# adaLN products of a float32 transformer trunk on VectorE and GpSimd with sums on ScalarE, weight transfers queued behind the main weights, and hidden activations in a ring of seven blocks

## The chip, the cores and the metric

The kernel runs on one core of a Trainium2 chip. The metric is the device time of one execution in microseconds (us), median over runs. TensorE (PE) does the matrix products, VectorE (DVE), ScalarE (ACT) and GpSimd (POOL) the elementwise work, and SyncE (SP) issues most transfers.

## The reference

Two layers of a diffusion transformer step, all in float32, on 384 tokens of width 1024. Each layer adds a gated half-step FFN, a mixer (differential attention, latent attention, a state-space scan called S5) and a second half-step FFN. Shift, scale and gate of each come from the adaLN product, a vector times a 1024 x 9216 matrix for each of two condition vectors:

```python
def adaln(cvec, l, p):
    m = jax.nn.silu(cvec) @ p['w_ada'][l] + p['b_ada'][l]
    return m.reshape(cvec.shape[0], N_MOD, D_MODEL)

def trunk_layer(x, mod, l, p, pos, ctx):
    sh1, sc1, g1, sh2, sc2, g2, sh3, sc3, g3 = [mod[:, i, None, :] for i in range(N_MOD)]
    nw = p['norm_w'][l]
    x = x + 0.5 * g1 * swiglu(modulate(rms_norm(x, nw[0]), sh1, sc1), p['ffn_w_in'][l, 0], p['ffn_w_out'][l, 0])
    m, new_ctx = mixer(modulate(rms_norm(x, nw[1]), sh2, sc2), l, p, pos, ctx)
    x = x + g2 * m
    x = x + 0.5 * g3 * swiglu(modulate(rms_norm(x, nw[2]), sh3, sc3), p['ffn_w_in'][l, 1], p['ffn_w_out'][l, 1])
    return x, new_ctx
```

`trunk_layer` runs for the prompt's 128 tokens with `c_ctx` and for the sample's 256 with `c`; the kernel takes both groups together, so each modulation has two columns.

## The kernel before

Activations lie transposed, 128 partitions x 8 blocks x 384 tokens. Every large product is exact to float32 by a split in two: ScalarE copies a weight block to `whi` (rounded), VectorE subtracts to get `wlo`, and `mm3` does three matmuls, whi x hi, whi x lo, wlo x hi. There are three buffers for raw weights and two for each split half, so a split can run at most one half block ahead of its matmuls. Weights come by SyncE, 1 MB at a time.

An FFN has 22 "up" blocks and 16 "down" blocks. An up block is two half blocks of 24 matmuls; behind it `up_post` copies a bias (`bb`), multiplies by the norm (`t`, out of PSUM), applies SiLU and the gate product (`sl`, ScalarE and VectorE in turn), and splits the result into `hidh` and `hidl`. Up and down alternate by `QUARTERS`: twelve ups, four downs, five ups, four downs, five ups, eight downs. The last downs of a stage also make the norm and the input of the next.

The adaLN products are cut into 64 units of 1 MB of weights (the first 8 MB are made in the start, apart). `ada_steps` makes them as steps in a list, `fillers`, and `fill` pops one after each up or down or attention step. A unit before is a load in SyncE's queue into one of the `raw` buffers and a run of small float32 matmuls on TensorE with the 2-column condition `conds` (`adaps`, L293); at the end of a group the sums are transposed (`adapt`) and added into `adaT`. Together with them, in the first FFN of a layer pair, go the steps of `s5_prep` (tables `big`, `Otab`, on VectorE and GpSimd). GpSimd otherwise does some `wlo` in the mixers. The units stand thus: 12 in the first FFN (called FFN00 here), 32 in mixer 0, 2 in FFN01 and 2 in FFN10 (second FFN of layer 0, first of layer 1), 16 in mixer 1, none in FFN11.

A scheduler of the framework puts the instructions of each engine into one fixed order; an engine runs its own list strictly in that order.

Of the kernel before, what the change touches and what calls it, by code (L numbers as in the profile page):

```python
# [31 lines left out]
YB = 8  # L32
# [33 lines left out]
def _layout(inp):  # L66
# [5 lines left out]
    wa = w[:, :, :8192].reshape(2, 8, 128, 4, 2048).transpose(0, 3, 1, 2, 4).reshape(2, 32, 128, 2048)  # L72
    wb = w[:, :, 8192:].reshape(2, 4, 2, 128, 1024).transpose(0, 1, 3, 2, 4).reshape(2, 4, 128, 2048)
    d['wada'] = np.concatenate([wa, wb], 1)
    for z in range(2):
        wc = w[:, :, 4096 + 1024 * z:5120 + 1024 * z].reshape(2, 4, 2, 128, 1024).transpose(0, 1, 3, 2, 4)
        d['wada'][:, 16 + 4 * z:20 + 4 * z] = wc.reshape(2, 4, 128, 2048)
    d['wada'][0, :8] = w[0, :, :2048].reshape(8, 128, 2, 8, 128).transpose(3, 1, 0, 2, 4).reshape(8, 128, 2048)
# [98 lines left out]
def trunk(ctx, tc, I, O):  # L177
# [100 lines left out]
    def ada_steps(l, g):  # L278
        w = 512 if g in (0, 1, 3) else 256
        units = w // 64  # L280
        row = int(8 * g)
        st = {}

        def unit(u):
            raw = load(I['wada'][l, row + u])
# [156 lines left out]
    def ffn(l, i, h, norm, gate, after, quiet=0, started=()):  # L442
        hh, hl = h
        fp = cur['fp']
        with cur['stack']:
            hq = {}

            def new_quarter(q):
                hq[q] = (fp.tile([128, 6, NT], FR, tag="hidh", name="hidh", bufs=2),
                         fp.tile([128, 6, NT], FR, tag="hidl", name="hidl", bufs=2))  # L450

            st = {}

            def up_post(j, ps):
                q = [n for n, (a, c) in enumerate(QUARTERS) if a <= j < a + c][0]
                if q not in hq:
                    new_quarter(q)
                dh, dl = hq[q]
                jj = j - QUARTERS[q][0]
# [39 lines left out]
            def down(q, m2):  # L499
# [4 lines left out]
                dh, dl = hq[q]  # L504
                for z in range(2):
                    w = split(raw[:, :, z, :], n, 128)
                    for k in range(n):
                        mm3(ps[z][:, :NT], w[0][:, k, :], w[1][:, k, :], dh[:, k, :], dl[:, k, :],
                            k == 0, k == n - 1)
# [1017 lines left out]
```

## Time and profile before

| | before |
|---|---|
| median of 3 runs | 1704.24 us (1701.77 to 1705.44) |
| the profiled execution's own time | 1711.13 us |
| span of its trace | 1708.8 us |
| PE busy | 1662.6 us, 97% |
| DVE busy | 1100.3 us, 64% |
| ACT busy | 690.3 us, 40% |
| POOL busy | 158.0 us, 9% |

A busy share is over the whole span; the span lies a few microseconds under the execution's own time, the rest being start and end of the program. The stages of the trace: start until 50 us, FFN00 to 340, mixer 0 to 594, FFN01 to 888, FFN10 to 1171, mixer 1 to 1413, FFN11 to 1696.

### The profile page before, as it was taken

The page shows a single profiled execution, that of the slowest core. Times are in us where ns is not written, and L with a number is a line of the kernel's source. Part 1 is how long each engine was busy: PE and PEld are TensorE (multiplying, and loading weights), DVE is VectorE, ACT ScalarE, POOL GpSimd, SP SyncE. Part 2 cuts the span into 40 slices and gives each one's busy share as a digit, 9 for nine tenths or more (in the row PEclk, how much of TensorE's full clock was granted, in tenths as well). Part 3 has the DMA queues.
Part 4 walks back from the last instruction along what each step waited for, and adds up shares of the span by engine and source line. Part 5 has one row for each costly group of instructions (what it writes and reads, how often), then busy time and mean ns, then how long its engine had stood idle before and what let it go on. Part 6 is the DMA issues. An engine that isn't in the chain of part 4 may idle for free.

```text
span 1708.8 us, 26147 instructions
## 1 busy us (share of the span) xinstructions
PE 1662.6 (97%) x10144; PEld 1502.8 (88%) x10144; DVE 1100.3 (64%) x2752; ACT 690.3 (40%) x1295; POOL 158.0 (9%) x220
## 2 busy tenths in 40 slices
PE   7999999999999999999999999999999999999997
PEld 6888999998545899999999999999964589999997
DVE  5974576757456788587576555557844766555555
ACT  4332343533455533333344333335234654333333
POOL 1210110013001400000000000001301040000000
PEclk9999999999999999999999999999998999999999
DMA  9564542544457443354253343435345123333432
GB/s 377 189 217 165 137 149 96 160 157 142 172 225 278 152 155 133 110 140 136 87 172 141 120 138 109 139 99 178 135 151 188 37 94 129 124 124 111 136 102 83
DMA packets 45931, 251.47 MB, mean 147 GB/s; under 512 B 5600, under 2 KB 10576, under 8 KB 23920
## 3 DMA queue, kind: packets, MB, share of 16 engines
q1 hardware_dynamic: 41360, 241.12, 40.9%
q0 software_dynamic: 2144, 4.54, 1.1%
q10 hardware_dynamic: 2304, 4.15, 0.8%
q8 instruction: 79, 1.29, 0.3%
q14 instruction: 44, 0.36, 0.1%
HBM read 246.73 MB, written 3.05 MB: 146 GB/s over the span
## 4 chain that ended last, share of the span: by engine, by line
PE 89%; DVE 5%; DMA 2%; ACT 2%; issue 1%; POOL 0%; SPq 0%; DVEq 0%; ACTq 0%
PE up L239 14%; PE up L241 14%; PE up L240 14%; PE down L241 7%; PE down L239 7%; PE down L240 7%; PE adaps L293 4%; PE pj L239 2%; PE sc L1208 2%; PE pj L241 2%; PE pj L240 2%; PE wtp L1165 1%; PE pout L239 1%; PE pout L241 1%; PE pout L240 1%
## 5 line engine op out<-in xcount | busy, mean ns | idle before, releaser
L234 ACT ACTIVATE whi<-raw 128x1024 fp32r<-128x1024 f32 (+3 forms) x360 | 332.5, 925 | 661.6 <-PE up L240 335.6
L239 PE MATMUL up<-hh,whi 128*128 128x386 f32 x1408 | 474.7, 342 | 7.8 <-ACT whi L234 4.0
L241 PE MATMUL up<-hh,wlo 128*128 128x386 f32 x1408 | 479.3, 341 | 0.7 <-DVE wlo L213 0.6
L240 PE MATMUL up<-hl,whi 128*128 128x386 f32 x1408 | 479.1, 341 | 0.0
L213 DVE TENSOR_TENSOR wlo<-raw,whi 128x1024 fp32r<-128x1024 f32 (+2 forms) x318 | 347.8, 1094 | 50.0 <-ACT whi L234 47.2
L239 PEld LDWEIGHTS up<-hh,whi 128*128 128x128 f32 x1408 | 266.5, 190 | 15.6 <-ACT whi L234 5.3
L241 PEld LDWEIGHTS up<-hh,wlo 128*128 128x128 f32 x1408 | 266.2, 189 | 9.4 <-DVE wlo L213 2.7
L240 PEld LDWEIGHTS up<-hl,whi 128*128 128x128 f32 x1408 | 266.7, 189 | 1.5 <-issue 1.1
L241 PE MATMUL down<-hidh,wlo 128*128 128x384 f32 x704 | 236.6, 336 | 0.0
L239 PE MATMUL down<-hidh,whi 128*128 128x384 f32 x704 | 236.0, 335 | 0.0
L240 PE MATMUL down<-hidl,whi 128*128 128x384 f32 x704 | 235.5, 335 | 0.0
L231 DVE SCALAR_TENSOR_TENSOR xTt<-down,gate,xTt 128x256 f32<-128x256 f32 (+1 forms) x256 | 95.1, 414 | 115.0 <-PE down L241 114.9
L466 DVE COPY bb<-up 128x2 f32<-128x2 f32 x176 | 27.8, 159 | 189.7 <-PE up L241 189.3
L241 PEld LDWEIGHTS down<-hidh,wlo 128*128 128x128 f32 x704 | 132.2, 188 | 1.1 <-issue 0.6
L239 PEld LDWEIGHTS down<-hidh,whi 128*128 128x128 f32 x704 | 132.2, 188 | 1.0 <-ACT whi L234 0.8
L240 PEld LDWEIGHTS down<-hidl,whi 128*128 128x128 f32 x704 | 132.3, 188 | 0.0
L213 DVE TENSOR_TENSOR t<-up,R 128x384 f32<-128x384 f32 x176 | 95.6, 549 | 3.3 <-ACT R L234 3.2
L293 PE MATMUL adaps<-raw,conds 128*32 128x256 f32 (+1 forms) x704 | 88.2, 503 | 5.0 <-DMA raw<-in_wada 5.0
L239 PE MATMUL pj<-hh,whi 128*128 128x386 f32 (+1 forms) x240 | 84.9, 355 | 0.9 <-ACT whi L234 0.7
L241 PE MATMUL pj<-hh,wlo 128*128 128x386 f32 (+1 forms) x240 | 83.3, 348 | 0.0
L240 PE MATMUL pj<-hl,whi 128*128 128x386 f32 (+1 forms) x240 | 83.1, 348 | 0.0
L234 ACT ACTIVATE hidh<-sl 128x384 fp32r<-128x384 f32 x88 | 46.1, 524 | 91.1 <-DVE sl L231 91.1
(268 smaller groups left out, 1988.5 us busy)
## 6 DMA issues: line engine op xcount, KB each, us to landing
raw<-in_wfi SPq DMA_DIRECT2D x85, 1024.0 KB, 4.9
raw<-in_wada SPq DMA_DIRECT2D x64, 1024.0 KB, 5.0
raw<-in_wfo SPq DMA_DIRECT2D x32, 768.0 KB, 4.3
raw<-in_wfo SPq DMA_DIRECT2D x32, 640.0 KB, 4.0
raw<-in_win SPq DMA_DIRECT2D x14, 1024.0 KB, 4.9
araw<-in_wada SPq DMA_DIRECT2D x8, 1024.0 KB, 9.8
raw<-in_wout SPq DMA_DIRECT2D x16, 512.0 KB, 3.5
wr<-in_wfi SPq DMA_DIRECT2D x8, 384.0 KB, 9.7
```

The lines of the kernel that those rows point to most:

```text
L213: return (eng or V).tensor_tensor(out, a, b, op=op)
L231: return V.scalar_tensor_tensor(out, a, s, b, op0=op0, op1=op1)
L234: S.activation(out, a, f, **k)
L239: T.matmul(out, whi, xhi, start=first, stop=False)
L240: T.matmul(out, whi, xlo, start=False, stop=False)
L241: marks.append(T.matmul(out, wlo, xhi, start=False, stop=last).ins)
L293: T.matmul(ps[32 * q:32 * q + 32, 0:w], conds[:, k, :], raw[:, c0:c0 + w], start=(k == 0), stop=(k == 7))
L466: V.tensor_copy(bb[:, z], ps[z][:, NT:NT + 2])
L1165: T.transpose(pt[:, kt * 128:(kt + 1) * 128], w[:, kt * 128:(kt + 1) * 128], ident)
L1208: T.matmul(sc, qT[p, self.b, t * 128:(t + 1) * 128], kT[p, self.b, self.k0:self.k0 + n], start=True, stop=True)
```

## The change

Each unit becomes two blocks of 128 output columns x 1024, laid out so that the output column is the partition. For each block VectorE multiplies it by the row `crow` of condition `c` into a tile `prod` (one buffer), GpSimd multiplies it in place by the row of `c_ctx`, and ScalarE sums each product along the free dimension while copying it (`accum_out`); VectorE then adds the four sums to the bias. The blocks lie in tiles `araw` (three buffers of their own). One of a unit's two loads stands in SyncE's queue and is issued after the last load of a main weight, the other in ScalarE's queue behind the unit's last sum. `crow` (1 MB, both conditions repeated on all partitions) is loaded and passed through SiLU once.

Besides: the hidden activations of an FFN lie in a ring of seven blocks instead of quarters, and up and down alternate by `UPS` (seven ups, four downs, six, four, six, four, three, four); the first down of the last quarter takes its last block's matmuls after those of both halves; two S5 transfers go from GpSimd's queue to ScalarE's. The units stand at 12 in FFN00, 16 in mixer 0, 8 in FFN01, 12 in FFN10, 16 in mixer 1, none in FFN11; the scheduler takes the products of one more unit forward from the mixer into FFN00.

```diff
+UPS = ((0, 7), (7, 13), (13, 19), (19, 22))
+RING = 7
+ADA = ((0, 8, 8), (0, 16, 4), (0, 20, 4), (0, 24, 8), (0, 32, 4),
+       (1, 0, 8), (1, 8, 8), (1, 16, 4), (1, 20, 4), (1, 24, 8), (1, 32, 4))
...
+    def ada_load(eng, behind=None):
+        if ablocks:
+            l, b = ablocks.pop(0)
+            raw = wp.tile([128, 1024], F32, tag="araw", name="araw", bufs=3)
+            with tc.issue_after(behind) if behind else nullcontext():
+                eng.dma_start(raw, I['wada'][l, b // 2, :, b % 2])
+            ahead.append((l, b, raw))
+
+    def ada_first(behind):
+        nc.scalar.dma_start(crow.rearrange("p c n -> p (c n)"), I['crow'])
+        act(crow, crow, AF.Silu)
+        ada_load(nc.sync, behind)
+        ada_load(nc.sync, behind)
+
+    def ada_steps(l, row, units):
         def unit(u):
-            raw = load(I['wada'][l, row + u])
...
-                for q in range(4):
-                    c0 = kk * 1024 + q * w
-                    T.matmul(ps[32 * q:32 * q + 32, 0:w], conds[:, k, :], raw[:, c0:c0 + w],
-                             start=(k == 0), stop=(k == 7))
...
+            ada_load(nc.sync, cur['load'])
+            b0 = 2 * (row + u)
+            s1 = sp.tile([128, 2, 2], F32, tag="as1", name="as1", bufs=2)
+            for z in range(2):
+                l_, b, raw = ahead.pop(0)
+                assert (l_, b) == (l, b0 + z)
+                prod = wp.tile([128, 1024], F32, tag="prod", name="prod", bufs=1)
+                mul(prod, raw, crow[:, 0])
+                act(prod, prod, AF.Copy, accum_out=s1[:, z, 0:1])
+                mul(raw, raw, crow[:, 1], G)
+                a = S.activation(raw, raw, AF.Copy, accum_out=s1[:, z, 1:2])
+            ada_load(nc.scalar, a.ins)
+            add(adaT[l][:, b0:b0 + 2, :], s1, bada[:, l, b0:b0 + 2, None].broadcast_to([128, 2, 2]))
...
-            for j in range(max(1, len(started)), 12):
-                up(j)
-                if j >= quiet:
-                    fill_after()
-            for q in range(4):
+            for q, (a, b) in enumerate(UPS):
+                for j in range(max(a, 1, len(started)), b):
+                    up(j)
+                    if j >= quiet:
+                        fill_after()
                 for m2 in range(4):
                     down(q, m2)
...
-    fillers += g1[:SKIP] + [both(f, g) for f, g in zip(g1[SKIP:], prep)] + inter(ada_steps(0, 2), prep[8 - SKIP:])
-
-    N1, N2 = 16, 18
+    ada = [ada_steps(*a) for a in ADA]
+    fillers += ada[0][:4] + [both(f, g) for f, g in zip(ada[0][4:] + ada[1], prep)] + prep[8:]
+
+    N1, N2 = 0, 8
```

VectorE before, an up block of FFN10 (`raw` is the main weight block, `up` the two sums in PSUM):

```order
L466 COPY bb_9569<-up_9519 128x2
L213 TENSOR_TENSOR t_9570<-up_9519,R_9319 128x384
L213 TENSOR_TENSOR wlo_9585<-raw_9582,whi_9584 128x1024
L466 COPY bb_9569<-up_9520 128x2
L213 TENSOR_TENSOR t_9570<-up_9520,R_9319 128x384
L213 TENSOR_TENSOR wlo_9589<-raw_9582,whi_9588 128x1024
L231 SCALAR_TENSOR_TENSOR sl_9575<-t_9570,bb_9569,sl_9575 128x256
L231 SCALAR_TENSOR_TENSOR sl_9575<-t_9570,bb_9569,sl_9575 128x128
L213 TENSOR_TENSOR hidl_9292<-sl_9575,hidh_9291 128x384
```

VectorE in the changed kernel, an up block of FFN10 with a unit:

```order
L460 COPY bb_9954<-up_9903 128x2
L213 TENSOR_TENSOR t_9955<-up_9903,R_9518 128x384
L213 TENSOR_TENSOR hid_9863<-sl_9870,hid_9863 128x384
L213 TENSOR_TENSOR wlo_9986<-raw_9983,whi_9985 128x1024
L213 TENSOR_TENSOR prod_10266<-araw_10195,crow_84 128x1024
L460 COPY bb_9954<-up_9904 128x2
L213 TENSOR_TENSOR t_9955<-up_9904,R_9518 128x384
L213 TENSOR_TENSOR adaT1_83<-as1_10197,sm_69 128x4
L213 TENSOR_TENSOR wlo_9990<-raw_9983,whi_9989 128x1024
L213 TENSOR_TENSOR prod_10271<-araw_10208,crow_84 128x1024
L231 SCALAR_TENSOR_TENSOR sl_9960<-t_9955,bb_9954,sl_9960 128x256
L231 SCALAR_TENSOR_TENSOR sl_9960<-t_9955,bb_9954,sl_9960 128x128
```

Each `wlo` now has a product behind it, and the add of the sums stands among them. GpSimd, whose list in this stage held only the 128x2 casts and differences of `hh` and `hl`, has 24 multiplies 128x1024 of `araw` there.

ScalarE in the changed kernel, about one unit in FFN10:

```order
L234 ACTIVATE prod_10130,as1_10129<-prod_10130 128x1024
L234 ACTIVATE whi_9895<-raw_9893 128x1024
L234 ACTIVATE hid_9773<-sl_9780 128x384
L308 ACTIVATE araw_10057,as1_10129<-araw_10057 128x1024
L234 ACTIVATE prod_10135,as1_10129<-prod_10135 128x1024
L234 ACTIVATE whi_9899<-raw_9893 128x1024
L308 ACTIVATE araw_10070,as1_10129<-araw_10070 128x1024
L287 DMA araw_10140<-in_wada 128x1024
```

The four sums and the unit's second load lie between the splits; none of these rows but `whi` and `hid` was there before.

SyncE in the changed kernel, the downs of FFN00 (in brackets the engines whose work a load waits for):

```order
L246 DMA raw_1290<-in_wfo 128x1536 [waits DMAHW6_49,DVE_49]
L287 DMA araw_1223<-in_wada 128x1024 [waits DMAHW0_49,Activation_49]
L246 DMA raw_1373<-in_wfo 128x1536 [waits DMAHW1_49,DVE_49]
L287 DMA araw_1342<-in_wada 128x1024 [waits DMAHW3_49,Activation_49]
L246 DMA raw_1454<-in_wfo 128x1536 [waits DMAHW4_49,DVE_49]
L287 DMA araw_1425<-in_wada 128x1024 [waits DMAHW6_49,Activation_49]
L287 DMA araw_1506<-in_wada 128x1024 [waits DMAHW0_49,Activation_49]
L246 DMA raw_1532<-in_wfi 128x2048 [waits DMAHW1_49,DVE_49]
```

Loads of `araw` that wait for ScalarE now stand ahead of loads of main weights in the one queue.

## Rows read from the trace of the kernel before

**Rows 1.** The chain of work that ended last, shares by engine.

```profile
PE 89%; DVE 5%; DMA 2%; ACT 2%; issue 1%; POOL 0%; SPq 0%; DVEq 0%; ACTq 0%
```

**Rows 2.** Busy time by stage: PE, PEld, DVE, ACT, POOL, granted clock, DMA share, GB/s.

```profile
0.00:50.00 50.00, 38.21 (x398) 34.30 (x398) 32.06 (x151) 20.06 (x44) 4.90 (x19) 1.00 0.93 353
50.00:340.00 290.00, 289.37 (x1704) 268.64 (x1703) 201.89 (x488) 108.70 (x174) 35.79 (x53) 1.00 0.48 157
340.00:594.00 254.00, 245.19 (x1606) 175.14 (x1606) 157.26 (x464) 111.64 (x278) 52.74 (x52) 0.98 0.52 187
594.00:888.00 294.00, 291.72 (x1726) 287.39 (x1725) 216.34 (x524) 117.52 (x188) 7.86 (x24) 1.00 0.41 132
888.00:1171.00 283.00, 283.00 (x1632) 280.61 (x1631) 168.63 (x336) 109.10 (x168) 4.11 (x17) 1.00 0.39 131
1171.00:1413.00 242.00, 232.06 (x1477) 175.30 (x1476) 151.18 (x441) 111.05 (x278) 51.62 (x52) 0.94 0.36 127
1413.00:1696.00 283.00, 280.71 (x1600) 279.48 (x1600) 166.34 (x326) 111.00 (x168) 1.00 (x5) 1.00 0.34 114
```

**Rows 3.** Timeline of PE at one adaLN unit: start, duration, operation, count.

```profile
91.31 1.06 PE L293 MATMUL adaps<-raw,conds 128*32 128x512 f32 x8
```

**Rows 4.** Timeline of VectorE at bare up and down blocks; in brackets idle before.

```profile
1024.28 0.16 DVE L466 COPY bb<-up 128x2 f32<-128x2 f32 x1 [2.11 <-PE up L241]
1032.76 0.16 DVE L466 COPY bb<-up 128x2 f32<-128x2 f32 x1 [0.29 <-PE up L241]
...
1071.83 0.74 DVE L231 SCALAR_TENSOR_TENSOR xTt<-down,gate,xTt 128x256 f32<-128x256 f32 x2 [1.40 <-PE down L241]
...
1078.07 0.74 DVE L231 SCALAR_TENSOR_TENSOR xTt<-down,gate,xTt 128x256 f32<-128x256 f32 x2 [1.46 <-PE down L241]
```

**Rows 5.** Groups by shape on VectorE: count, busy us, mean ns, idle before.

```profile
L213 DVE TENSOR_TENSOR wlo<-raw,whi 128x1024 fp32r<-128x1024 f32 x188 | 231.3, 1231 | 47.8 <-ACT whi L234 47.2
L213 DVE TENSOR_TENSOR t<-up,R 128x384 f32<-128x384 f32 x176 | 95.6, 549 | 3.3 <-ACT R L234 3.2
L213 DVE TENSOR_TENSOR wlo<-raw,whi 128x768 fp32r<-128x768 f32 x66 | 63.9, 969 | 2.0
...
L213 DVE TENSOR_TENSOR hidl<-sl,hidh 128x384 fp32r<-128x384 f32 x88 | 49.4, 561 | 32.3 <-ACT hidh L234 32.3
...
L231 DVE SCALAR_TENSOR_TENSOR sl<-t,bb,sl 128x256 f32<-128x256 f32 x88 | 43.0, 488 | 0.6 <-ACT sl L234 0.6
...
L231 DVE SCALAR_TENSOR_TENSOR sl<-t,bb,sl 128x128 f32<-128x128 f32 x88 | 30.4, 346 | 0.0
```

**Rows 6.** The same on GpSimd, its subtraction of a full half block.

```profile
L213 POOL TENSOR_TENSOR wlo<-raw,whi 128x1024 fp32r<-128x1024 f32 x10 | 24.1, 2413 | 69.5 <-ACT whi L234 54.3 <-PE adaps L293 15.2
```

**Rows 7.** Timeline, GpSimd and VectorE side by side in mixer 0.

```profile
383.98 2.40 POOL L213 TENSOR_TENSOR wlo<-raw,whi 128x1024 fp32r<-128x1024 f32 x1 [9.99 <-ACT whi L234]
...
384.40 2.26 DVE L213 TENSOR_TENSOR qT<-ra,rb 128x256 f32<-128x256 f32 x1
```

**Rows 8.** The operations on that tile: ns least/median/most, times of first and last.

```profile
L213 DVE TENSOR_TENSOR qT<-ra,rb x6: 417/2258/3547, 384.4 to 1239.8; 128x256 f32<-128x256 f32 x6
```

**Rows 9.** Timeline, GpSimd and VectorE side by side in FFN00.

```profile
73.59 1.30 POOL L213 TENSOR_TENSOR big<-s5c,p 128x288 f32<-128x288 f32 x1 [0.62 <-DVE Otab L231]
...
74.34 1.63 DVE L213 TENSOR_TENSOR wlo<-raw,whi 128x1024 fp32r<-128x1024 f32 x1
```

**Rows 10.** Busy time in shorter stretches, columns as in rows 2.

```profile
50.00:100.00 50.00, 49.99 (x286) 43.01 (x285) 49.13 (x135) 20.05 (x33) 18.27 (x20) 1.00 0.52 190
100.00:150.00 50.00, 50.00 (x278) 42.36 (x278) 27.50 (x59) 16.89 (x26) 1.00 (x1) 1.00 0.52 179
...
1300.00:1350.00 50.00, 45.57 (x253) 24.44 (x254) 28.23 (x104) 25.48 (x79) 3.71 (x4) 0.85 0.33 121
```

**Rows 11.** Groups by shape on ScalarE, a split's copy and an accumulator's read.

```profile
L234 ACT ACTIVATE whi<-raw 128x1024 fp32r<-128x1024 f32 x198 | 209.4, 1060 | 418.2 <-PE up L240 285.3 <-issue 50.0 <-PE down L240 36.4
...
L234 ACT ACTIVATION_READ_ACCUMULATOR e<-sc,nm 128x1 f32 x108 | 21.6, 200 | 0.0
```

More of the change, by code (lines that the diff above doesn't have):

```diff
@@ L31 @@
 AT5 = (0, 5)
-YB = 8
+YB = 7
 KO = (6, 7, 0, 1, 2, 3, 4, 5)
@@ L71, in _layout @@
     w = a['w_ada']
[L72 to L78, printed above, removed]
+    d['wada0'] = w[0, :, :2048].reshape(8, 128, 2, 8, 128).transpose(3, 1, 0, 2, 4).reshape(8, 128, 2048)
+    d['wada'] = w.transpose(0, 2, 1).reshape(2, 36, 2, 128, 1024).transpose(0, 1, 3, 2, 4)
     d['wfi'] = a['ffn_w_in'].reshape(2, 2, 8, 128, 2, NJ, 128).transpose(0, 1, 5, 3, 2, 4, 6).reshape(2, 2, NJ, 128, 2048)
@@ L245, in load @@
         with tc.issue_after(cur.pop('dma')) if 'dma' in cur else nullcontext():
-            nc.sync.dma_start(raw[:, :n], src)
+            cur['load'] = nc.sync.dma_start(raw[:, :n], src).ins
         return raw
@@ new lines, in trunk @@
+    crow = cst.tile([128, 2, 1024], F32, name="crow")
+    ablocks = [(l, 2 * (r + u) + z) for l, r, n in ADA for u in range(n) for z in range(2)]
+    ahead = []
+    def ada_load(eng, behind=None):
[5 more added lines that the diff above has]
+            ahead.append((l, b, raw))
@@ L445, in ffn @@
         with cur['stack']:
[L446 to L450, printed above, removed]
+            hid = {}
             st = {}
             def up_post(j, ps):
[L455 to L459, printed above, removed]
+                hid[j] = fp.tile([128, 2, NT], FR, tag="hid", name="hid", bufs=RING)
                 if 'R' not in st:
@@ L471, in up_post @@
                     stt(sl[:, a:b], t[:, 0, a:b], bb[:, 0, c:c + 1], sl[:, a:b], ALU.add, ALU.mult)
-                act(dh[:, jj, :], sl, AF.Copy)
-                st['last'] = sub(dl[:, jj, :], sl, dh[:, jj, :])
+                act(hid[j][:, 0], sl, AF.Copy)
+                st['last'] = sub(hid[j][:, 1], sl, hid[j][:, 0])
             def up_weights(j):
@@ L503, in down, with part @@
                 ps = [bank("down"), bank("down")]
[L504 to L508, printed above, removed]
+                w = {}
+                def part(z, ks):
+                    if z not in w:
+                        w[z] = split(raw[:, :, z, :], n, 128)
+                    for k in ks:
+                        x = hid[j0 + k]
+                        mm3(ps[z][:, :NT], w[z][0][:, k, :], w[z][1][:, k, :], x[:, 0], x[:, 1],
                             k == 0, k == n - 1)
+                cuts = (0, n - 1, n) if q == 3 and m2 == 0 else (0, n)
+                for a, b in zip(cuts, cuts[1:]):
+                    for z in range(2):
+                        part(z, range(a, b))
                 g = gate()
@@ L793, in s5_prep @@
         steps += [kext]
-        steps += [lambda d=d, hf=hf: gtab(d, hf) for d in range(2) for hf in range(4)]
+        steps += [lambda d=d, hf=hf: (gtab(d, hf), kwin() if (d, hf) == (0, 3) else None) for d in range(2) for hf in range(4)]
         steps += [etab]
@@ L1408, in start @@
                 nx += 1
-            raw = stp.tile([128, 2048], F32, tag="araw", name="araw", bufs=4)
-            nc.sync.dma_start(raw, I['wada'][0, k])
+            raw = stp.tile([128, 2048], F32, tag="araw0", name="araw0", bufs=4)
+            nc.sync.dma_start(raw, I['wada0'][k])
             wr = stp.tile([128, NF, 256], F32, tag="wr", name="wr", bufs=4)
@@ L1442, in trunk @@
     nc.scalar.dma_start(co[:, 128:], I['const'][:, 128:])
+    ada_first(cur['dma'])
     s5stack, P, prep = open_s5(0)
@@ L1509, in trunk @@
         (nc.sync if i % 2 else nc.scalar).dma_start(yv[:, a:b], xT[:, a:b])
-_NAMES = ('xT', 'wada', 'wfi', 'wfo', 'win', 'wout', 'wsm', 's5', 'small', 'lam', 'kc', 'vc', 'ckvc', 'kpec', 'const')
+_NAMES = ('xT', 'wada0', 'wada', 'crow', 'wfi', 'wfo', 'win', 'wout', 'wsm', 's5', 'small', 'lam', 'kc', 'vc', 'ckvc', 'kpec', 'const')
 def kernel(**inputs):
```

45 lines of the change are left out of this document (9 added, 36 removed).

## The prediction

> **What bounds the kernel now.** I read the chain of waits first: 89% of it is TensorE [rows 1]. The busy times by stage show why [rows 2]: in the four FFN stages TensorE works all but 1 to 3 us, while VectorE works 166 to 216 of about 285 us, ScalarE 109 to 118, and GpSimd 1 to 36. In the two mixers TensorE is idle 9 to 10 us and everything is closer together. So TensorE's own work is what sets the end, and taking work off it pays as long as nothing else gets late. The FFNs are periodic: a bare up block lasts 1032.76 - 1024.28 = 8.48 us, a bare down block 1078.07 - 1071.83 = 6.24 us [rows 4]. VectorE waits for TensorE at each half block there, 2.11 us ahead of the first `bb`. The room that an added operation has in a block is what is free on its engine within these 8.48 or 6.24 us.
>
> **What is removed.** A unit's matmuls take 1.06 us of TensorE [rows 3]; the pipelined end overlaps what follows, so I take 1.0. 64 units give 64 us, the transposes and sums of `adapt` some 3 more: about -67 us, if nothing takes their place.
>
> **What is added.** Per unit VectorE gets two 128x1024 products with both inputs in SBUF. The nearest row is its own `wlo` of that shape and kind, 1.23 us [rows 5]. GpSimd gets two of the same; its `wlo` takes 2.41 us [rows 6]. ScalarE gets four sums, each priced like `whi`, 1.06, with an accumulator read of 0.20 [rows 11]: 5.0 us, with a DMA issue some 5.4. If the three worked independently, there would be room: VectorE 2.5 us in a block.
>
> They don't. In mixer 0 GpSimd's `wlo` runs from 383.98 to 386.38; VectorE's small product `qT`, started at 384.40, lasts until 386.66, 2.26 us [rows 7], where the same operation takes 0.42 at best; its median over six is 2.26 [rows 8]. In FFN00 GpSimd's `big` ends at 73.59 + 1.30 = 74.89, and a `wlo` of 1.23 us that was started at 74.34 lasts 1.63, to 75.97 [rows 9]: 1.08 us, its whole work, behind the other's end. So of a GpSimd multiply and a VectorE operation on SBUF one stands still until the other is done; their times add. Nothing in these rows shows them sharing. The Trainium skill (SBUF — State Buffer, "SBUF: two separate sides") says the same of a pair of ports that both engines use: an exclusive lock, held for a whole instruction, against a VectorE operation with two SBUF inputs if the GpSimd one reads SBUF. By that rule every GpSimd product here shuts out `prod`, `wlo`, `sl` and `hid`, and this trace agrees; read as engines of their own, the change would gain.
>
> I therefore count both engines as one resource. A unit takes 2 x 2.41 + 2 x 1.23 = 7.28 us of it. An up block needs besides 2 x 1.23 (`wlo`), 0.49 + 0.35 (`sl`), 0.56 (`hid`), 3.86 in all [rows 5]: 11.1 us with a unit, against 8.48 of TensorE. A down block needs 2 x 0.97 besides, 9.2 us against 6.24. The split has two buffers, so TensorE can hide one late half block and then waits each time: the `wlo` is late next.
>
> **The FFNs.** By the order of the changed kernel units go with nearly every step until they are used up; after that TensorE is the bound again and nothing is given back. So per stage I sum this resource over the stretch with units and subtract TensorE's time there.
>
> - FFN00: 13 units 94.6; 7 up blocks 27.0; 4 down blocks 7.7; the ends of the three up blocks of the start 4.2; the S5 tables. In before, these make VectorE busy 49.13 of the first 50 us of this stage against 27.50 in the next 50, and GpSimd 18.27 against 1.00 [rows 10]; 21.6 + 17.3, with what the two wait for each other counted once: 37. Sum 170.5. TensorE: 7 x 8.48 + 4 x 6.24 and some 7 for the last blocks of the start, 91.6. Excess 79; less 13 for the removed matmuls, less 4 for the half block that the split is ahead: +62.
> - FFN01: 8 units 58.2; 5 ups 19.3; 4 downs 7.7; of the 50 us that VectorE has here beyond FFN11 (216.34 - 166.34 [rows 2]: the S5 tables of layer 1) about 29 by the order: 114. TensorE 67.4. 47 - 2 - 4 = +41.
> - FFN10: 12 units 87.4; 8 ups 30.9; 4 downs 7.7: 126. TensorE 92.8. 33 - 2 - 4 = +27.
> - FFN11 has no units: 0.
>
> That is +130. VectorE's other operations read PSUM (`bb`, `t`, the residual sum `xTt`). Beside GpSimd they may run (1.4 us an up block, 1.5 a down block by [rows 4, 5], some 50 us over the three stretches), beside VectorE's own work they can't. Bounds 0 and +50; GpSimd holds two thirds of a unit's time, but VectorE's fixed order often brings a blocked operation first: half, +25.
>
> **The mixers.** TensorE loses 32 and 16 us of matmuls and a little of `adapt`, so it would need about 220 and 224 us. VectorE has 157.3 + 39.4 (32 products) - 1.9 = 194.8 and 151.2 + 36.9 - 1.2 = 186.9; GpSimd gets 77 and 72 us more. If six tenths of that hold VectorE up, it is occupied 241 and 230 us of 254 and 241, in stages where the softmax passes between VectorE, ScalarE and TensorE many times. So the gain is eaten; I take +10 together. Bounds: only the removed matmuls, -52; all of GpSimd's time a hold-up, 272 and 259 us, +35.
>
> **The rest.** `crow` is 1 MB more in the start, where transfers run at 353 GB/s, 0.93 of the engines busy [rows 2]: 3 us, and the first products stand in VectorE's list ahead of the last two `wlo` of the start, behind loads that come last: +3. Other transfers are the same bytes at half the DMA engines' time: 0, hidden by the raw buffers while these are filled in time. Seven ups instead of twelve ahead of the first down, the ring and the last down's cut move the same matmuls: 0; without cover each would cost a wait for `hid` at a turn, a few tenths.
>
> **Sum:** 130 + 25 + 10 + 3 = +168 us. Made against the profiled execution (1711 us, 7 above the median), it is a difference, so I add it to the median: 1704 + 168 = **1872 us**. The low end of the unknown terms gives 130 + 0 - 52 + 3 = +81, 1785; the high end 130 + 50 + 35 + 3 = +218, 1922.
>
> **The rivals.**
>
> 1. *The clock falls too.* For: the only stretch above with a granted clock under 1.00 is one where TensorE had gaps: 0.85 in 1300 to 1350, busy 45.57 of 50 [rows 10]; in the FFNs, without gaps, it is 1.00 [rows 2]. With units TensorE would work only 54 to 74% of a stretch. Against: its gaps would be short, 1 to 1.5 us a half block. If it is at 1.2 of its two levels, 1.2 and 2.4 GHz, over these stretches, TensorE needs twice its time, 184, 135 and 186 us against 170, 114 and 126 of the shared resource: +14, +21, +60. Time 1872 + 95 = 1967. The Trainium skill (TensorE: Matmul & The Clock Gate, "HAM oscillation — how this bites in real kernels") tells of a loop whose waits between bursts brought the clock down at every tile; by that rule the 1967 would be the forecast. No row here shows it at gaps so short, so I leave it a rival.
> 2. *A GpSimd product holds VectorE up for about half its time only* (it starts behind a PSUM reader, or VectorE happens to wait for ScalarE). Per unit 4.87 us: FFN00 139 - 92 - 17 = +31, FFN01 95 - 67 - 6 = +21, FFN10 97 - 93 - 6 = -2; mixers -10, start +3: +43, 1747.
> 3. *The two engines hardly hinder each other: faster.* Place: FFN10. It has room for 92.8 + 4 - 38.6 = 58 us, 4.9 a unit, of which VectorE's products take 2.46: if a unit's GpSimd products hold VectorE up for less than 2.4 of their 4.82 us, TensorE stays the bound there and all is gain but for ScalarE. That has 109.1/283 x 92.8 = 36 us of its own and 12 x 5.4 = 65, 101 against 93: +8; in FFN00 104 against 92, +13. -67 + 21 + 3 = -43, 1661. Against it speak rows 7 to 9.
> 4. *A queue binds instead.* A main load stands in SyncE's queue behind an `araw` load that waits for ScalarE's sum, and that for GpSimd's product; with one `prod` VectorE waits for ScalarE. It comes on top of the forecast, and only if a unit lags by more than the three raw buffers cover, two to three blocks. Worth some 20 us in the mixers, where five such loads stand in a row: inside the range.
>
> **Chances.** Forecast, with rival 4 inside it: 0.60. Rival 1: 0.15. Rival 2: 0.15. Rival 3: 0.10. The range reaches from rival 2 to rival 1: 1745 to 1970; the likeliest case's own is 1785 to 1922. A difference under 0.2%, about what a measurement of this kernel can tell from none, would need rival 2 and 3 to meet by chance: 0.02. Faster: 0.10. Slower: 0.88.
>
> **What the new profile would show.** If I am right: in FFN00, FFN01 and FFN10 TensorE idle in the unit stretches, waiting for VectorE's `wlo` above all; up blocks there 11 us apart, 8.5 after; `wlo` and `prod` with means well above 1.23 us, GpSimd's products at or above 2.41; FFN11 unchanged at 283 us. If rival 1: granted clock near half in those stretches. If rival 3: `wlo` at 1.23 us beside GpSimd's products and blocks of 8.5 us. I would be wrong most simply if the locked pairs in the rows of before are special to their shapes, or if VectorE's order puts its waits for TensorE just where GpSimd works.

## The result, and the profile after

The changed kernel takes 1919.82 us (median of 4 runs, 1918.03 to 1920.99) against 1704.84 before: a ratio of 1.1261, 95% interval 1.1236 to 1.1285. It is slower by 215 us; forecast were +168, 1872, with a range to 1970.

The page of the changed kernel, its span, busy times and the chain of waits:

```profile
span 1918.7 us, 25721 instructions
...
PE 1663.0 (87%) x9408; PEld 1536.1 (80%) x9408; DVE 1436.3 (75%) x2900; ACT 959.6 (50%) x1797; POOL 497.5 (26%) x344
...
PE 58%; DVE 26%; issue 7%; DMA 4%; ACT 4%; POOL 1%; SPq 0%; DVEq 0%; ACTq 0%; POOLq 0%
```

TensorE's share of the chain fell from 89% [rows 1] to 58%, VectorE's rose from 5% to 26%. Busy time by stage of the changed kernel (columns as in [rows 2]):

```profile
0.00:52.00 52.00, 36.90 (x384) 32.01 (x385) 32.65 (x149) 23.14 (x47) 8.11 (x20) 0.97 0.99 383
52.00:391.00 339.00, 293.31 (x1584) 282.13 (x1583) 280.21 (x522) 162.43 (x274) 104.66 (x75) 0.92 0.42 133
391.00:681.00 290.00, 229.62 (x1271) 183.38 (x1270) 230.90 (x489) 176.62 (x401) 135.33 (x85) 0.83 0.32 107
681.00:1017.00 336.00, 300.48 (x1692) 289.80 (x1691) 258.93 (x547) 152.10 (x251) 51.03 (x38) 0.96 0.42 137
1017.00:1333.00 316.00, 291.56 (x1599) 284.05 (x1598) 237.53 (x369) 159.95 (x264) 66.71 (x40) 0.97 0.43 147
1333.00:1621.00 288.00, 226.37 (x1274) 182.76 (x1273) 222.48 (x473) 173.00 (x393) 130.12 (x82) 0.83 0.31 103
1621.00:1905.00 284.00, 281.09 (x1596) 278.74 (x1595) 166.73 (x326) 111.12 (x169) 1.55 (x6) 1.00 0.34 115
```

Every stage with units is longer: the two mixers 290 and 288 us against 254 and 242, FFN00 339 against 290 (here with the start's last blocks in it), FFN01 336 against 294, FFN10 316 against 283; FFN11, which has none, is unchanged within 1 us. So the loss lies where the units lie, also in the mixers.

What TensorE waits for in the FFNs is above all `wlo`, as the prediction had it. The third matmul of each triple, in before and in the changed kernel (behind the second bar, its idle time in us):

```profile
L241 PE MATMUL up<-hh,wlo 128*128 128x386 f32 x1408 | 479.3, 341 | 0.7 <-DVE wlo L213 0.6
L241 PE MATMUL down<-hidh,wlo 128*128 128x384 f32 x704 | 236.6, 336 | 0.0
```

```profile
L241 PE MATMUL up<-hh,wlo 128*128 128x386 f32 x1408 | 484.8, 345 | 37.7 <-DVE wlo L213 37.7
...
L241 PE MATMUL down<-hid,wlo 128*128 128x384 f32 x704 | 244.7, 349 | 35.6 <-DVE wlo L213 35.6
```

A stretch of FFN10 with units, and one of the same stage after the last unit:

```profile
1055.00:1105.00 50.00, 42.06 (x215) 40.76 (x216) 50.00 (x56) 34.86 (x59) 24.58 (x9) 0.93 0.54 185
...
1250.00:1300.00 50.00, 50.00 (x287) 50.00 (x286) 29.26 (x58) 17.52 (x25) 0.00 (x0) 1.00 0.40 129
```

With units VectorE is never idle, 50.00 of 50, and TensorE 42.06; without, TensorE 50.00 and VectorE 29.26. Inside the first of these, one up block of VectorE's timeline, and GpSimd's in the same time:

```profile
1062.34 0.15 DVE L460 COPY bb<-up 128x2 f32<-128x2 f32 x1
...
1064.08 1.22 DVE L213 TENSOR_TENSOR wlo<-raw,whi 128x1024 fp32r<-128x1024 f32 x1
1065.21 2.89 DVE L231 SCALAR_TENSOR_TENSOR sl<-t,bb,sl 128x256 f32<-128x256 f32 x2
1068.02 1.21 DVE L213 TENSOR_TENSOR prod<-araw,crow 128x1024 f32<-128x1024 f32 x1
...
1069.23 0.54 DVE L213 TENSOR_TENSOR t<-up,R 128x384 f32<-128x384 f32 x1
1069.69 3.08 DVE L213 TENSOR_TENSOR wlo<-raw,whi 128x1024 fp32r<-128x1024 f32 x1
...
1073.17 0.14 DVE L460 COPY bb<-up 128x2 f32<-128x2 f32 x1
```

```profile
1064.29 3.26 POOL L213 TENSOR_TENSOR araw<-araw,crow 128x1024 f32<-128x1024 f32 x1 [4.61 <-DVE prod L213]
1069.31 2.38 POOL L213 TENSOR_TENSOR araw<-araw,crow 128x1024 f32<-128x1024 f32 x1 [1.76 <-DVE bb L460]
```

The block, from its second `bb` to the next block's, lasts 1073.17 - 1062.34 = 10.83 us; the sum had 11.1. The five blocks about it, 1053.48 to 1106.85, last 8.9 to 12.0 us, 10.7 in the mean. GpSimd's second product ends at 1069.31 + 2.38 = 1071.69, and the `wlo` that was started at 1069.69 ends at 1072.77, 1.08 us behind it, the same 1.08 as in [rows 9]. The pair `sl`, 0.74 us in a bare block, takes 2.89. GpSimd's first product was started at 1064.29 while a `wlo` ran to 1065.30, and took 3.26 instead of 2.38. The `t` at 1069.23 reads PSUM and takes its 0.54 beside GpSimd. No other `t` of the kernel takes longer either (least, median and most in ns):

```profile
L213 DVE TENSOR_TENSOR t<-up,R x176: 538/547/559, 71.3 to 1883.5; 128x384 f32<-128x384 f32 x176
```

### The profile page after: what moved, and what is told of

Same layout as the page of the kernel before. It is cut to its first block, busy times and chain, and to the rows that moved or that the text cites. A ratio compares the mean times of both kernels' runs of the same rounds, so it can differ in the third digit from the quotient of the medians.

```text
span 1918.7 us, 25721 instructions
## 1 busy us (share of the span) xinstructions
PE 1663.0 (87%) x9408; PEld 1536.1 (80%) x9408; DVE 1436.3 (75%) x2900; ACT 959.6 (50%) x1797; POOL 497.5 (26%) x344
## 4 chain that ended last, share of the span: by engine, by line
PE 58%; DVE 26%; issue 7%; DMA 4%; ACT 4%; POOL 1%; SPq 0%; DVEq 0%; ACTq 0%; POOLq 0%
PE up L240 10%; PE up L239 10%; PE up L241 10%; PE down L241 5%; PE down L239 5%; PE down L240 5%; DVE prod L213 5%; DVE wlo L213 4%; DMA araw<-in_wada 3%; DVE sl L231 2%; DVE big L213 2%; PE pout L241 1%; DVE rsu L213 1%; PE pout L239 1%; PE sc L1248 1%
## 5 line engine op out<-in xcount | busy, mean ns | idle before, releaser
L213 POOL TENSOR_TENSOR araw<-araw,crow 128x1024 f32<-128x1024 f32 x128 | 334.1, 2610 | 328.9 <-DVE prod L213 224.9
L213 DVE TENSOR_TENSOR wlo<-raw,whi 128x1024 fp32r<-128x1024 f32 (+2 forms) x318 | 374.2, 1178 | 38.6 <-ACT whi L234 36.7
L241 PE MATMUL down<-hid,wlo 128*128 128x384 f32 x704 | 244.7, 349 | 35.6 <-DVE wlo L213 35.6
L239 PE MATMUL down<-hid,whi 128*128 128x384 f32 x704 | 243.5, 348 | 10.4 <-ACT whi L234 6.0
L240 PE MATMUL down<-hid,whi 128*128 128x384 f32 x704 | 242.9, 345 | 7.6 <-DVE hid L213 7.6
L213 DVE TENSOR_TENSOR prod<-araw,crow 128x1024 f32<-128x1024 f32 x128 | 173.7, 1357 | 32.7 <-DMA araw<-in_wada 22.6
L234 ACT ACTIVATE prod<-prod 128x1024 f32<-128x1024 f32 x128 | 135.1, 1055 | 104.2 <-DVE prod L213 100.0
L241 PEld LDWEIGHTS down<-hid,wlo 128*128 128x128 f32 x704 | 136.6, 194 | 43.1 <-DVE wlo L213 42.7
L308 ACT ACTIVATE araw<-araw 128x1024 f32<-128x1024 f32 x128 | 134.5, 1051 | 41.6 <-POOL araw L213 41.5
L239 PEld LDWEIGHTS down<-hid,whi 128*128 128x128 f32 x704 | 136.6, 194 | 16.2 <-ACT whi L234 11.0
L240 PEld LDWEIGHTS down<-hid,whi 128*128 128x128 f32 x704 | 137.1, 195 | 8.8 <-DVE hid L213 8.8
L231 DVE SCALAR_TENSOR_TENSOR sl<-t,bb,sl 128x256 f32<-128x256 f32 (+1 forms) x176 | 102.1, 617 | 0.6 <-ACT sl L234 0.6
```

What stands on the lines that cost most here:

```text
L213: return (eng or V).tensor_tensor(out, a, b, op=op)
L231: return V.scalar_tensor_tensor(out, a, s, b, op0=op0, op1=op1)
L239: T.matmul(out, whi, xhi, start=first, stop=False)
L240: T.matmul(out, whi, xlo, start=False, stop=False)
L241: marks.append(T.matmul(out, wlo, xhi, start=False, stop=last).ins)
L308: a = S.activation(raw, raw, AF.Copy, accum_out=s1[:, z, 1:2])
```

## The experiments

The length of each stage, from its first large matmul to that of the next stage (the start: from the beginning to the end of the start's last up block), in us, with each run's time; they are worked out from TensorE's records of each trace, while the times are medians. A trace is one execution; that of before took 1711.13 us, 6 above its median, so a few us against the first row mean little, and e4's row, with the same matmuls in an execution of 1707.39, is the closer one to compare with. The times of e1, e2, e3, e5, e6, e8, e10 and e13 are single runs, the others medians of four to ten.

| run | start | FFN00 | mixer 0 | FFN01 | FFN10 | mixer 1 | FFN11 | time |
|---|---|---|---|---|---|---|---|---|
| before | 55 | 285 | 255 | 294 | 283 | 241 | 283 | 1704.84 |
| changed | 67 | 323 | 290 | 336 | 316 | 288 | 284 | 1919.82 |
| e1, all products on VectorE | 64 | 302 | 285 | 319 | 302 | 274 | 284 | 1844.68 |
| e2, no GpSimd products | 61 | 288 | 261 | 308 | 293 | 257 | 284 | 1766.61 |
| e13, no VectorE products | 64 | 300 | 283 | 324 | 302 | 264 | 284 | 1835.84 |
| e3, no products | 61 | 283 | 246 | 296 | 289 | 243 | 284 | 1716.76 |
| e5, transfers only | 58 | 272 | 236 | 294 | 291 | 236 | 284 | 1687.66 |
| e4, ring only | 56 | 284 | 251 | 297 | 284 | 235 | 284 | 1707.32 |
| e6, sums on VectorE | 65 | 298 | 285 | 322 | 302 | 275 | 284 | 1847.34 |
| e7, half units | 64 | 302 | 255 | 294 | 293 | 237 | 284 | 1741.79 |
| e9, the same, held | 62 | 292 | 256 | 294 | 286 | 232 | 284 | 1720.31 |
| e10, changed, held | 61 | 316 | 299 | 324 | 312 | 295 | 284 | 1905.42 |
| e8, matmuls put back | 65 | 373 | 289 | 334 | 315 | 290 | 284 | 1964.87 |
| e12, by stage | 56 | 283 | 239 | 300 | 283 | 236 | 284 | 1698.30 |

The theory: a GpSimd multiply and a VectorE operation on SBUF exclude each other, and this shared time, with VectorE's own work, sets the stretches with units. The rivals: the engines hardly hinder each other and something else binds (ScalarE's sums, the queues); the lower clock; the ring.

**e1. GpSimd's products on VectorE.**

```diff
-                mul(raw, raw, crow[:, 1], G)
+                mul(raw, raw, crow[:, 1])
```

> The changed kernel (1920 us) with the c_ctx products on VectorE too, GpSimd without any. If a GpSimd product shuts VectorE out for its whole length (my theory), a unit now takes 4 x 1.23 = 4.9 us of the shared resource, not 7.3: some 2.4 us less for each of the 33 units in FFN stretches, about -70, time 1830 to 1870, though VectorE has 157 us more to do. If the engines hardly hinder each other (rival), VectorE's added work makes it slower: 1950 to 2000.

Measured 1844.68, as the theory had it: VectorE gets 163 us more to do and the program is 75 us shorter. The place is not quite the one forecast: by the table some 56 of the 75 lie in the start and the FFNs, where the sum had 70, and 19 in the mixers. In its trace:

```profile
L213 DVE TENSOR_TENSOR wlo<-raw,whi 128x1024 fp32r<-128x1024 f32 x188 | 232.7, 1238 | 32.6 <-ACT whi L234 32.3
...
L213 DVE TENSOR_TENSOR araw<-araw,crow 128x1024 f32<-128x1024 f32 x128 | 162.7, 1271 | 0.5
```

`wlo` is back at 1238 ns; in the changed kernel these lines read:

```profile
L213 DVE TENSOR_TENSOR wlo<-raw,whi 128x1024 fp32r<-128x1024 f32 x188 | 247.3, 1316 | 37.0 <-ACT whi L234 36.7
L213 DVE TENSOR_TENSOR prod<-araw,crow 128x1024 f32<-128x1024 f32 x128 | 173.7, 1357 | 32.7 <-DMA araw<-in_wada 22.6 <-ACT prod L234 8.9 <-ACT sl L234 0.4
...
L213 POOL TENSOR_TENSOR araw<-araw,crow 128x1024 f32<-128x1024 f32 x128 | 334.1, 2610 | 328.9 <-DVE prod L213 224.9
```

One product took GpSimd 2.6 us, with waits for VectorE in it, and VectorE does it in 1.27.

**e2 and e13. One of the two products left out.** In e2 ScalarE sums the plain weights in place of GpSimd's product, in e13 in place of VectorE's.

```diff
-                mul(raw, raw, crow[:, 1], G)
```

> The changed kernel with the GpSimd products left out (the c_ctx sums are then those of the plain weights, which changes that half of the modulations); transfers, sums and VectorE's products stay. Theory: 4.8 us a unit gone from the shared resource, the FFN stretches are TensorE's again, mixers near before: 1690 to 1730. Rival (ScalarE's sums, the single prod tile or the queues are what costs): 1850 or more.

```diff
-                mul(prod, raw, crow[:, 0])
-                act(prod, prod, AF.Copy, accum_out=s1[:, z, 0:1])
+                act(prod, raw, AF.Copy, accum_out=s1[:, z, 0:1])
```

> The changed kernel with VectorE's products left out (the sums for c are those of the plain weights, all modulations of the sample change), GpSimd's stay. If GpSimd's products shut out VectorE's main work (wlo, sl, hid: my theory), most of the added time stays: 1830 to 1870. If the two products of a unit only stand in each other's way (rival), it comes down to about the run without GpSimd's, 1767 or less.

e2 measured 1766.61: GpSimd's products are worth 153 us, far from the rival's 1850, but 37 us above the upper end of what I expected. e13 measured 1835.84: with GpSimd's alone most of the loss stays, so they shut out VectorE's main work, not only `prod`. That e2 stayed above 1730 asked for what else there is.

**e3 and e5. No products; then no sums either.**

```diff
-                mul(prod, raw, crow[:, 0])
-                act(prod, prod, AF.Copy, accum_out=s1[:, z, 0:1])
-                mul(raw, raw, crow[:, 1], G)
+                act(prod, raw, AF.Copy, accum_out=s1[:, z, 0:1])
                 a = S.activation(raw, raw, AF.Copy, accum_out=s1[:, z, 1:2])
```

> Both products left out, ScalarE sums the plain weights twice (all modulations change); transfers, their queue places and the four sums of a unit stay. Theory: what is left is TensorE without the adaLN matmuls and a little of ScalarE: 1640 to 1680. Rival, queues or ScalarE bind: over 1720, with the mixers longer than before (254 and 242 us).

```diff
-                act(prod, raw, AF.Copy, accum_out=s1[:, z, 0:1])
-                a = S.activation(raw, raw, AF.Copy, accum_out=s1[:, z, 1:2])
+                a = V.tensor_copy(s1[:, z, :], raw[:, 0:2])
```

> Products and sums both left out: of each arrived block VectorE copies two columns (all modulations change); transfers and their queue places stay. The run without products lost all of the 67 us that the removed matmuls should give. If ScalarE's sums took them (my theory after that run; worked out, 21 us in the FFNs and the rest in the mixers), 1640 to 1665. If the loads' places in the queues or the 1 MB of crow took them (rival), 1695 to 1720 again.

Neither expectation held. e3, 1716.76, lies between both. e5, 1687.66, is 29 us below e3: the sums cost that much where nothing else binds. But 67 us of matmuls are gone in e5 and only 18 come back (1687.66 against 1705.99 for the kernel before in the same set of runs). (The 67 is the prediction's estimate.) The table says where: FFN00 gives its 13 us; mixer 0 gives 18 against before, 15 against e4, where 32 units of matmuls are out; mixer 1 gives nothing against e4, 236 with none and 235 with 16 units. FFN10 is 8 us longer than before with transfers alone. Busy time by stage, e5's mixers:

```profile
330.00:567.00 237.00, 208.22 (x1276) 169.19 (x1275) 157.14 (x491) 108.62 (x275) 53.82 (x53) 0.94 0.39 133
...
1152.00:1388.00 236.00, 209.90 (x1272) 169.26 (x1270) 152.20 (x471) 109.09 (x274) 51.80 (x52) 0.93 0.37 125
```

and e4's mixer 1, with the matmuls:

```profile
1172.00:1407.00 235.00, 226.27 (x1470) 172.84 (x1469) 149.00 (x438) 109.88 (x276) 51.84 (x52) 0.96 0.37 129
```

TensorE is busy 210 and 226 us in nearly the same time, 236 and 235. But e5 doesn't show alone that the matmuls lay in gaps, for there VectorE's list waits for loads of `araw` that come late, 80.5 us in all (`as` is the copy that stands in place of products and sums); then in mixer 0, FFN10 and mixer 1 (us in total, times, longest):

```profile
L304 DVE COPY as<-araw 128x2 f32<-128x2 f32 x128 | 31.5, 250 | 80.9 <-DMA araw<-in_wada 80.5
```

```profile
DVE as L304 <- DMA araw<-in_wada: 21.3, 12, 5.7
...
DVE as L304 <- DMA araw<-in_wada: 29.6, 9, 4.9
...
DVE as L304 <- DMA araw<-in_wada: 21.0, 10, 6.9
```

For mixer 1 the trace of e9 (below) settles it, since that stage has there no matmuls of units, and of products only the last three blocks left over from FFN10:

```profile
1190.00:1422.00 232.00, 208.43 (x1273) 167.78 (x1271) 160.53 (x449) 109.83 (x277) 51.96 (x52) 0.94 0.19 63
```

It takes 232 us against 235 with 16 units of matmuls: these did lie in gaps, and late loads can account for some 4 us of e5's 236 at most. For mixer 0 and FFN10 no run separates the two. e5 and the changed kernel also have what e4 lacks: the two S5 transfers in ScalarE's queue, seven instead of eight buffers for one kind of S5 tile (`YB`), and a setting of the DMA scratch size; these were not tried alone.

**e4. The ring alone**, the FFN function of the changed kernel in the kernel before.

```diff
-    fillers += g1[:SKIP] + [both(f, g) for f, g in zip(g1[SKIP:], prep)] + inter(ada_steps(0, 2), prep[8 - SKIP:])
+    fillers += [both(f, g) for f, g in zip(g1[0::2], g1[1::2])] + inter(ada_steps(0, 2), prep)
```

> The kernel before with the FFN function of the changed one alone (ring of seven, order of ups and downs, the cut of the last down); the adaLN matmuls stay on TensorE, two units to each of the first four steps since the first down comes earlier. Theory: the same matmuls in another order, 1700 to 1712. Rival: waits for hid at each turn, 16 turns of over 1 us, 1720 or more.

1707.32, ratio 1.0003 (0.9992 to 1.0014): nothing, as forecast.

**e6. Products with their sum in one instruction on VectorE**, ScalarE and GpSimd free of units.

```diff
+                V.scalar_tensor_tensor(prod, raw, 1.0, crow[:, 0], op0=ALU.mult, op1=ALU.mult, accum_out=s1[:, z, 0:1])
+                a = V.scalar_tensor_tensor(raw, raw, 1.0, crow[:, 1], op0=ALU.mult, op1=ALU.mult, accum_out=s1[:, z, 1:2])
```

> All products on VectorE, each with its sum in the same instruction (an accumulator output); nothing of a unit on GpSimd or ScalarE, else as changed. With VectorE's products and ScalarE's sums in e1 it was 1845. If VectorE alone sets the stretches with units, ScalarE's release gives little: 1815 to 1845. If ScalarE's sums cost on top of it, 1750 to 1800.

1847.34, the same as e1 within 3 us, 2 above the end of the first case's range. So beside all products on VectorE the sums on ScalarE cost nothing; they cost 29 us where there are no products.

**e8. Matmuls put back in each unit**, to raise the clock.

```diff
+            for kk in range(2):
+                for q in range(4):
+                    T.matmul(ps[32 * q:32 * q + 32, 0:256], conds[:, kk, :], crow[:, 0, 256 * q:256 * q + 256],
+                             start=(kk == 0), stop=(kk == 1))
```

> The changed kernel with the removed matmuls' like put back in each unit, on data that is always there, their result unused: 1.0 us of TensorE a unit. If the lower granted clock (0.92 on the whole, 0.83 in the mixers) costs time by itself, work in the gaps raises it and the time falls by 10 us or more, under 1910. If TensorE only waits there (my theory), it lies in the gaps or costs a little: 1915 to 1950.

1964.87, above both. These matmuls depend on no load, and the scheduler moved them all forward: of their 1024 records in the trace 704 lie in FFN00, which grew to 373 us, 272 in mixer 0, the rest in the start, none behind. So as a whole it doesn't tell the rivals apart. What reached mixer 0 raised its clock; busy times of e8 there:

```profile
438.00:727.00 289.00, 245.91 (x1547) 184.25 (x1546) 232.91 (x487) 176.87 (x402) 135.57 (x85) 0.88 0.32 107
```

0.88 against 0.83, and 289 us against 290: no gain in that stage from a higher clock, with 23 us of added matmuls in it that cost nothing either.

**e7, e9 and e10. Half units, and a place in the order.** In e7 a step gets one block, both its products on VectorE with the sum inside, only in FFN00 (12 units) and FFN10 (20); the other 32 units are matmuls as before. In e9 the first product of a block may stand in VectorE's list only behind the last `wlo` of its step; e10 is the changed kernel with that rule for both engines.

```diff
+            with tc.issue_after(cur['sub']):
+                V.scalar_tensor_tensor(prod, raw, 1.0, crow[:, 0], op0=ALU.mult, op1=ALU.mult, accum_out=s1[:, 0:1])
+            V.scalar_tensor_tensor(raw, raw, 1.0, crow[:, 1], op0=ALU.mult, op1=ALU.mult, accum_out=s1[:, 1:2])
```

> A version after the theory: half a unit to a step (2 x 1.23 us of VectorE, with the sum in the same instruction, beside 5.3 us of 8.5 in an up block), only in FFN00 (12 units) and FFN10 (20 units); all other units stay matmuls as before. Theory: 32 us of matmuls gone and VectorE just fits, less some 10 in FFN00 where the gate's units must come in four steps: 1675 to 1690. Rival (any added operation in VectorE's order delays the splits): 1705 or more.

> e7 with the first product of a half unit allowed into VectorE's list only behind the last wlo of its step; in e7 the list held seven half units in a row ahead of the small operations of the first norm, and TensorE waited 16 us for these. Theory (room in a block is there, the order of the list wasted it): 1675 to 1700. Rival (what VectorE does beside the splits delays them in any order): 1720 or more.

> The changed kernel with the same rule: the products of both engines come in their lists only behind the last wlo of their step. If the added time is that of the shared resource (my theory), a better place takes away the bunches only, 10 to 30 us: 1885 to 1910. If it was the bunching of the products ahead of splits that cost (rival), under 1860.

e7 measured 1741.79, ratio 1.0208 (1.0189 to 1.0227), against my theory. One wait makes up 16 of the 36 us lost (total, times, longest):

```profile
PEld pr L429 <- DVE tiny L236: 16.3, 1, 16.3
```

The list held products in a row ahead of the small operations of the first norm. e9 measured 1720.31, 1.0086 (1.0073 to 1.0099): 21 us less by order alone, yet at the edge of what the rival gave, not where my theory had it. The table separates it: FFN10 hides 18 and a half units for 3 us (286 against 283), three blocks run over into mixer 1, and that is still 9 shorter than before and 3 shorter than in e4; the start and FFN00, where eight half units must come in four steps beside the S5 tables, lose 13. e10 measured 1905.42, in the range of the theory: in the changed kernel order is worth 14 us in all. By the table it takes 30 us off the start and the FFNs and adds 16 to the mixers.

**e12. Units by stage.** FFN00 keeps its matmuls; mixer 0 keeps 16 of its 32 units and mixer 1 its 16; 8 units go to FFN01 and 12 to FFN10 as held half units on VectorE; `crow` is loaded in mixer 0.

```diff
+    fillers += [both(f, g) for f, g in zip(g1[0::2], g1[1::2])] + inter(ada_pe(0, 2), prep)
...
+            q = hv[0]
+            fillers += prep[:1] + [both(f, g) for f, g in zip(q[:7], prep[1:8])] + inter(q[7:], prep[8:])
...
+            q = hv[1]
+            fillers += [both(q[0], q[1]), both(q[2], q[3])] + q[4:]
```

> Units placed by what the stages showed. FFN00 and the start as before but in the ring's order (that alone was 1.0003 of before); mixer 0 with 16 instead of 32 units of matmuls, since the run with transfers only has this stage 18 us shorter without any; mixer 1 with its 16, which gave back nothing there; the other 20 units as half units on VectorE, held behind the splits, 8 in FFN01 and 12 in FFN10, where e9 hid 20 at 3 us. Theory: -15 in mixer 0, +3 to +8 in the two FFNs: 1693 to 1702. Rival (FFN01 with its S5 tables has no room on VectorE): 1706 or more.

1698.30, as expected, ratio 0.9956 to before (0.9943 to 0.9970): 0.4% faster than before, and 222 us faster than the changed kernel. Busy times of its two FFNs with units:

```profile
579.00:880.00 301.00, 293.46 (x1697) 286.17 (x1696) 250.99 (x611) 117.40 (x187) 4.57 (x22) 1.00 0.48 152
880.00:1166.00 286.00, 284.25 (x1616) 282.48 (x1615) 223.38 (x458) 109.13 (x171) 5.73 (x20) 1.00 0.49 163
```

VectorE takes 223 of 286 us in FFN10 and TensorE still works nearly all of it; in FFN01, with the S5 tables, 251 of 301, and the stage is 7 us longer than before. Mixer 0 gave 16 us against before, 12 against e4.

## Why the prediction was right, and where only its sum was

**The mechanism: right.** GpSimd's products shut VectorE out and the reverse; the block of 10.83 us against 11.1, the `wlo` that ends 1.08 us behind GpSimd, e1 and e13 show it. The rule of the Trainium skill (SBUF — State Buffer, "SBUF: two separate sides"), an exclusive lock held for a whole instruction, agrees with these rows. Rival 2 (half the hold-up) and rival 3 (none) fall: for FFN10 rival 2 had -2 us, where +33 came, and rival 3 had the whole kernel faster.

**The FFNs, +155 forecast: +115 measured** (39, 42, 33 and 1 by the table's unrounded lengths). FFN01 and FFN10 came near the sum of the shared time, +41 and +27. The term that failed is the half of VectorE's PSUM readers, +25: they ran beside GpSimd. In the trace 21 of the `t` and 28 of the operations that make `xTt` out of `down` overlap a GpSimd product, and none takes longer than without one (551 and 484 ns at most). FFN00 was counted too high, 62 against 39, or 51 with the start; why, these runs don't show.

**The start, +3 forecast: +12 measured.** Of `crow` and the transfers it is 3 (e5); the other 9 came with the products and their sums. There the sum counted the products only, not what GpSimd does to the small operations. VectorE's timeline of the changed kernel has a difference `hl` of the last start blocks at 2.48 us instead of 0.35, and GpSimd's:

```profile
49.51 2.48 DVE L231 SCALAR_TENSOR_TENSOR hl<-xTt,mod,hh 128x128 fp32r<-128x128 f32 x1
```

```profile
49.38 2.46 POOL L213 TENSOR_TENSOR araw<-araw,crow 128x1024 f32<-128x1024 f32 x1 [3.27 <-ACT ad L234]
```

**The mixers, +10 forecast with bounds to +35: +82 measured.** This is the term that was mis-sized. The runs split it: GpSimd's products 61 (changed less e2), VectorE's 28 (e2 less e3), the sums 16 (e3 less e5), all else -23 (e5 less before), where I had -52 for the matmuls alone. Taken in the other order, with e13, the products are 58 and 32. Two things were missed. In mixer 1 the matmuls lay in TensorE's gaps, so their removal gave little; in mixer 0, where 15 to 18 of 32 us came back, gaps and late loads are not told apart. And I compared VectorE's total with the stage's length, where much of VectorE's work is tiny operations in chains, the softmax's among them, each of which now can wait for a whole GpSimd product: a multiply of one column, usually 0.16 us, in mixer 0:

```profile
563.01 2.33 DVE L213 TENSOR_TENSOR rsu<-rsu,su 128x1 f32<-128x1 f32 x1
```

with GpSimd's product beside it:

```profile
562.98 2.34 POOL L213 TENSOR_TENSOR araw<-araw,crow 128x1024 f32<-128x1024 f32 x1 [3.49 <-DVE rsu L1215]
```

All of its kind, in ns:

```profile
L213 DVE TENSOR_TENSOR rsu<-rsu,su x36: 148/159/2341, 521.9 to 1576.1; 128x1 f32<-128x1 f32 x36
```

Of these 36, ten overlap a GpSimd product, and they average 1.9 us; three reciprocals of one column, with one input, overlap one too and stay at 0.16 us. Counted over both mixers, VectorE's operations take 100 us more than at their usual (median) lengths, against 15 us in the kernel before; 55 of the 100 lie in operations that usually take under 0.4 us. That these delays, one behind the other, are what lengthens the stage is argued from this count and from e2; no run keeps GpSimd away from the tiny operations alone.

The three errors, -40, +9 and +72, partly cancel (the parts add to 209 us, the trace of before being 6 us above its median). That 1920 lies inside the likeliest case's own range, 1785 to 1922, is luck: the mixers alone are 47 us beyond their upper bound, and the FFNs' surplus hides most of it.

**The clock (rival 1): it fell, 0.92 on the whole, 0.83 in the mixers.** (The forecast's remark that one stretch alone was under 1.00 overlooks the mixers in [rows 2], 0.98 and 0.94.) A stretch all at the lower level would read 0.5, which rival 1 needs; the FFNs with units read 0.92 to 0.97 by stage. Within them it goes lower, in FFN00 (twice), FFN01 and FFN10:

```profile
112.00:142.00 30.00, 18.93 (x69) 16.11 (x68) 30.00 (x41) 16.12 (x30) 18.74 (x11) 0.69 0.37 123
142.00:178.00 36.00, 23.30 (x104) 21.68 (x104) 35.42 (x47) 17.90 (x31) 22.76 (x12) 0.78 0.48 158
755.00:815.00 60.00, 38.41 (x176) 34.43 (x177) 54.26 (x82) 30.83 (x52) 25.29 (x9) 0.80 0.42 140
1032.00:1060.00 28.00, 21.96 (x96) 20.35 (x97) 25.38 (x37) 18.72 (x33) 14.12 (x6) 0.76 0.48 166
```

In the two of FFN00, as in FFN10's at 0.93, VectorE is busy all or nearly all of the time and TensorE is not, so a lower clock of TensorE can have set little there; e8's mixer 0 gained nothing at 0.88. What the clock costs in the other two, where VectorE has 6 and 3 us free, was not separated.

**The queues (rival 4)** stay open. FFN10 with transfers alone is 8 us longer than before, and VectorE waits 29.6 us for late `araw` loads there. In the changed kernel it waits 22.6 us in all for `araw`, and by the profile's page loads of `araw` are 3% of the chain that ended last, some 58 us:

```profile
PE up L240 10%; PE up L239 10%; PE up L241 10%; PE down L241 5%; PE down L239 5%; PE down L240 5%; DVE prod L213 5%; DVE wlo L213 4%; DMA araw<-in_wada 3%; DVE sl L231 2%; DVE big L213 2%; PE pout L241 1%; DVE rsu L213 1%; PE pout L239 1%; PE sc L1248 1%
```

How much of that a better place for the loads would give back no run shows.

## What to carry to other kernels

Work that moves to GpSimd isn't beside VectorE's where both read SBUF and VectorE's operation takes two inputs from it, as here (one with an input in PSUM ran beside it): add their times, and price the blocker by its own length against the shortest operation in a chain behind it. Before removing work from the busiest engine ask, stage by stage, whether it lies in that engine's gaps, as 16 units did in mixer 1: there it costs almost nothing, and only stages that are really full give anything back. Room on an engine is used a little to a step, and only in an order that keeps the added work behind what the next engine waits for.

## What the runs showed of the hardware that was not expected

A VectorE product of 128x1024 with its sum in the same instruction took no longer than one without; reading the sum out adds 0.08 us. Its groups in e12, mean 1219 and 1220 ns, beside 1225 for the subtraction of that shape:

```profile
L218 DVE TENSOR_TENSOR wlo<-raw,whi 128x1024 fp32r<-128x1024 f32 x188 | 230.3, 1225 | 39.0 <-ACT whi L239 38.3
...
L315 DVE SCALAR_TENSOR_TENSOR araw<-araw,crow 128x1024 f32<-128x1024 f32 x40 | 48.8, 1220 | 0.2
L314 DVE SCALAR_TENSOR_TENSOR prod<-araw,crow 128x1024 f32<-128x1024 f32 x40 | 48.8, 1219 | 0.0
...
L314 DVE DVE_READ_ACCUMULATOR prod<-araw,crow 128x1 f32 x40 | 3.3, 83 | 0.0
```
